# The compressed branch's softmax of a hybrid decoder layer: 32x32 block turns on VectorE in place of 128x128 transposes on TensorE

## The chip, the core and the metric

The kernel is one launch on one core of a Trainium2 chip. A core has five engines that run their own instruction streams: TensorE (PE, matrix products from SBUF into PSUM; its weight loads are listed as PEld), VectorE (DVE), ScalarE (ACT), GpSimd (POOL) and SyncE (SP), which here only issues transfers (DMAs). The streams are tied together by semaphores alone. The metric is the device time of the launch in microseconds (us), as a median over runs; less is better.

## What is computed

The layer takes `x` (512 tokens, 1024 channels), projects it once to 5912 columns, runs two token mixers on the result, gates and merges them, projects back and normalises. Mixer B is a gated linear recurrence (HGRN2) in chunks. Mixer A is a sparse attention of 8 heads in 2 groups, with three branches that share the queries: a compressed branch, a selected branch and a window branch. The change touches the compressed branch. There the keys and values of 32 tokens at a stride of 16 are squeezed by a small network into 31 compressed keys and values, and each query attends to those whose block has ended:

```python
def masked_softmax(s, mask):
    s = jnp.where(mask, s.astype(jnp.float32), -jnp.inf)
    m = jnp.max(s, axis=-1, keepdims=True)
    m = jnp.where(jnp.isfinite(m), m, 0.0)
    p = jnp.exp(s - m)
    d = jnp.sum(p, axis=-1, keepdims=True)
    return p / jnp.where(d > 0, d, 1.0)
...
        sc = jnp.einsum('bghqd,bgnd->bghqn', qn, kc) * scale
        pc = masked_softmax(sc, cmp_end[None, :] <= t[:, None])
        o_cmp = jnp.einsum('bghqn,bgnd->bghqd', pc.astype(vc.dtype), vc)
...
        return gt[..., 0:1] * o_cmp + gt[..., 1:2] * o_slc + gt[..., 2:3] * o_win
```

`gt` are the sigmoid gates per token, head and branch. With 512 tokens every block of the selected branch is taken, so both other branches are full causal attention over 512 keys here.

## The kernel before

**Products.** Each fp32 operand is split into a high part, rounded to the format `fp32r`, and the low rest, and a product is three matmuls: high by high, high by low, low by high. The high part is a cast on ACT, the low part a subtraction on DVE (`split2`, line 171; `split_steps`, line 176; the weights in `weights`, lines 249 to 255: the cast at line 251, the subtraction at line 254). A projection tile (`proj`, line 296) is 24 matmuls of 512 columns; its weights come by one DMA of 512 KB into one of two `wraw` buffers, asked for three tiles ahead (`load`), and split two tiles ahead.

**Order.** The order of the work is written out by hand with a counter. `_Weave` (line 75) holds a list of running chains, each a Python generator. Every projection calls `weave.tick()` four times, so that a tick stands for six matmuls, and each chain whose time has come emits its next piece and says by `yield n` in how many ticks it goes on. A piece that a chain emits stands ahead of the tick's six matmuls. The numbers `n` are the table `D` (line 70). `claim(ticks)` (line 97) keeps two PSUM-hungry pieces apart: a chain that claims holds the weave for so many ticks, and the next one that wants to claim polls until then. The instructions of TensorE and all the DMAs on SP keep this program order. Those of DVE and ACT, except a few, are ordered when the program is built.

**Tiles in order.** Ticks are counted here from the first `proj_i` (line 884): ticks 0 to 15 are the four value tiles of mixer B, 16 to 87 the tiles of `SEQ` (line 39; four ticks each, the `v` pair eight), 88 to 151 the sixteen merge gates, and 152 to 183 the eight branch tiles (`BRANCH`, line 47). Then come the output products without ticks.

**Full attention.** `attn_scores` (line 671) works in units `u`: query block i = 3, 2 with one branch each, then i = 1, 0 with both, in two halves of heads (`ms`). Each half claims `e0` ticks, issues its score matmuls, has the masking (line 702) done by DVE and starts `soften` (line 710): the exponentials on ACT (line 718), after `e1` ticks the division and the gates (lines 723 to 738), after `e3` and `t0` the 32x32 turns on DVE (line 746) into `big`. After the second half and `t3` ticks 16 DMAs (line 757) move the turned blocks across partitions into `turn`, and `t1` ticks later a chain `values` (line 764) starts for each block of 128 keys, `t4` ticks apart. It casts the high part on ACT into one of three `t4` buffers, subtracts on DVE (both by `split_steps`, lines 177 and 179, `y` ticks apart), and `t2` ticks later issues four matmuls into `pso`. One unit must be spent before the next unit's 16 DMAs are issued (line 750).

**Compressed branch.** `cmp_scores` (line 623) computes the scores with the 32 keys (31 and an empty one) on partitions, four heads below each other, and the 512 queries along the free dimension, for two groups `g`. Both results are copied to SBUF, by ACT (line 634) and by DVE (line 635). `cmp_probs` (line 640), once for each group, claims, turns the scores to queries on partitions by four 128x128 transposes on TensorE (`transpose4`, line 385), adds the mask (line 645), does the softmax along the 32 keys and multiplies by the gate over the sum, claims again, turns back by four more transposes and copies the result to SBUF (line 664). `attn_sum` (line 793) waits for both groups, claims, multiplies with the compressed values and adds the branches.

**Gates.** `gates` (line 579) turns the gate logits of tokens on partitions into `gat`, and multiplies the compressed branch's by `rvalid`, which is 0 for the first 31 queries, which see no compressed key.

**Turning for RoPE.** `rope` (line 591) moves each query or key tile by four DMAs of 64 KB, on SP.

Of the kernel before, what the change touches and what calls it, by code (L numbers as in the profile page):

```python
# [9 lines left out]
F32 = mybir.dt.float32  # L10
# [3 lines left out]
ALU = mybir.AluOpType  # L14
# [4 lines left out]
P = 128  # L19
KT = DM // P  # L20
NEG = -1.0e30
# [28 lines left out]
def _columns(name):  # L50

    c = np.arange(_COLS[name], _COLS[name] + 128)
    if name[0] == "q" and name[1] != "b" or name[:2] == "za":
# [9 lines left out]
O_END = O_PEV + 16  # L63


K_ID, K_TRI, K_CM, K_RV, K_SM, K_COS, K_SIN, K_MASK, K_END = (
    0, 128, 256, 384, 388, 900, 1412, 1924, 2436)


D = dict(h0=6, h2=5, h3=14, h4=0, h5=7, h6=8, n0=6, n1=3, n2=4, c0=1, c1=3, c2=4, c3=3, r0=5, p0=5, p1=6, p2=2, s0=5,  # L70
         s2=11, s3=2, v0=10, v1=11, v2=5, v3=9, e0=4, e1=2, t0=5, t1=5, t2=4, t3=2, t4=1, a5=1, y=2, w0=1, w1=3,
         x0=0, x1=1, e2=0, e3=2, o0=2, o1=6, o2=4)


class _Weave:
# [32 lines left out]
def layer_kernel(ctx: ExitStack, tc: tile.TileContext, xT, xn, w0, wi, wf, wv, small, brow, consts,  # L108
                 w1, w2, wbr, wout, lng, lnb, out):
    nc = tc.nc  # L110
    V, A, G = nc.vector, nc.scalar, nc.gpsimd
# [13 lines left out]
    cst = ctx.enter_context(tc.tile_pool(name="cst", bufs=1))  # L125
    strm = ctx.enter_context(tc.tile_pool(name="strm", bufs=3))
    come = ctx.enter_context(tc.tile_pool(name="come", bufs=2))
    t2 = ctx.enter_context(tc.tile_pool(name="t2", bufs=59))
    t4 = ctx.enter_context(tc.tile_pool(name="t4", bufs=3))
# [8 lines left out]
    def T2(n=512, dt=F32):  # L138
        return t2.tile([P, n], dt, name="t2", tag="t2")
# [10 lines left out]
    def SM(n, name):  # L150
        return sm.tile([P, n], F32, name="sm_" + name, tag="sm")
# [4 lines left out]
    def PS():  # L156
        return pss.tile([P, 512], F32, name="pss", tag="pss")

    def PT():
        return pst.tile([P, 512], F32, name="pst", tag="pst")  # L160
# [15 lines left out]
    def split_steps(src, dst_hi, dst_lo):  # L176
        A.copy(dst_hi, src)  # L177
        yield D["y"]
        V.tensor_tensor(dst_lo, src, dst_hi.bitcast(F32), ALU.subtract)  # L179
# [14 lines left out]
    con = cst.tile([P, K_SM], F32, name="con")  # L194
# [50 lines left out]
    def split_later(i):  # L245
        if i < len(order) and i not in parts:
            weave.start(weights(i), D["w0"])

    def weights(i):
        hi = strm.tile([P, 1024], F32R, name="whi", tag="whi")  # L250
        A.copy(hi, raws[i])  # L251
        yield D["w1"]
        lo = strm.tile([P, 1024], F32R, name="wlo", tag="wlo")
        V.tensor_tensor(lo, raws[i], hi.bitcast(F32), ALU.subtract)  # L254
        parts[i] = hi, lo
# [6 lines left out]
        dma(t, consts[:, K_SM + 512 * i:K_SM + 512 * i + 512])  # L262
    ident = con[:, K_ID:K_ID + 128]
    tri = con[:, K_TRI:K_TRI + 128].bitcast(I32)
    cmask = con[:, K_CM:K_CM + 128].rearrange("p (i n) -> p i n", n=32)
    rvalid = con[:, K_RV:K_RV + 4]

    def bias(m):
# [18 lines left out]
    for m in range(4):  # L287
        s = T2()
# [5 lines left out]
    weave = _Weave()  # L294

    def proj(name):
        i = M_INDEX[name]
        load(i + 3)
        split_later(i + 2)
        hi, lo = parts[i]  # L300
        ps = PA()
        for kt in range(KT):
            if kt % 2 == 0:
                weave.tick()
            c = slice(128 * kt, 128 * kt + 128)
            T.matmul(ps, hi[:, c], xh[kt], start=kt == 0, stop=False)
            T.matmul(ps, hi[:, c], xl[kt], start=False, stop=False)
            T.matmul(ps, lo[:, c], xh[kt], start=False, stop=kt == KT - 1)
        return ps, 4 + i
# [26 lines left out]
    def proj_v():  # L336
# [3 lines left out]
        for tt in range(4):  # L340
            c = slice(128 * tt, 128 * tt + 128)
            ps = PA()
            for kt in range(KT):
# [9 lines left out]
                T.matmul(ps[:, 0:NV], xl[kt][:, c], hi, start=False, stop=kt == KT - 1)  # L353
            weave.start(values_of(tt, ps), D["x0"])
            if tt == 1:
# [4 lines left out]
    def values_of(tt, ps):  # L360
        v = T2(NV)
        V.tensor_tensor(v, ps[:, 0:NV], brv, ALU.add)
        yield D["y"]
        vd = vv[:, tt].rearrange("p b (g c) -> p b g c", c=64)
        v4 = v[:, 0:256].rearrange("p (b g c) -> p b g c", b=2, c=64)
        G.tensor_copy(gat[:, tt], v[:, 256:NV])
        vts.append(vv[:, tt])
        yield from split_steps(v4, vd[:, :, 0:4:3], vd[:, :, 1:3])
# [13 lines left out]
    def chunks(ap):  # L382
        return ap.rearrange("p (t c s) -> p t c s", c=2, s=64)

    def transpose4(src, n=4):
        ps = PT()
        for j in range(n):
            T.transpose(ps[:, 128 * j:128 * j + 128], src[:, 128 * j:128 * j + 128], ident)
        return ps
# [22 lines left out]
    def hgrn(h):  # L412
# [11 lines left out]
        for w, e in ((1, e2), (0, e1)):  # L424
            V.tensor_tensor(chunks(e), cm[:, w].unsqueeze(3).to_broadcast([P, 4, 2, 64]), bc, ALU.subtract)
        yield D["h2"]
        qp = T2()
# [109 lines left out]
    mvs, ready = [None, None], set()  # L537
# [37 lines left out]

    gat = cst.tile([P, 4, 24], F32, name="gat")
    gv = gat.rearrange("p i (h b) -> p i h b", b=3)

    def gates():
        while len(vts) < 4:  # L580
            yield 1
        gflat = gat.rearrange("p i c -> p (i c)")
        A.activation(gflat, gflat, AF.Exp, scale=-1.0)
        yield 1
        V.tensor_scalar(gflat, gflat, 1.0, 2.0, ALU.add, ALU.mult)
        V.reciprocal(gflat, gflat)
        V.tensor_tensor(gv[:, :, :, 0], gv[:, :, :, 0], rvalid.unsqueeze(2).to_broadcast([P, 4, 8]), ALU.mult)
        ready.add("gates")


    def rope(raw):
# [29 lines left out]
    PTc = {}  # L621

    def cmp_scores():

        while "cmp" not in ready or len(qraw) < 4:
            yield 1
        yield from weave.claim(2)
        pg = PS(), PS()
        for m in range(4):
            for g in range(2):  # L630
                gs = slice(64 * g, 64 * g + 64)
                T.matmul(pg[g][32 * m:32 * m + 32], kcB[gs], qraw[m][gs], start=True, stop=True)
        sT = T2(), T2()
        A.copy(sT[0], pg[0])
        V.tensor_copy(sT[1], pg[1])
        yield D["p2"]
        for g in range(2):
            weave.start(cmp_probs(g, sT[g]), 2 * g)

    def cmp_probs(g, src):  # L640
        yield from weave.claim(2)
        ps = transpose4(src)
        s = T2()
        s3 = s.rearrange("p (x n) -> p x n", n=32)
        V.tensor_tensor(s.rearrange("p (i m n) -> p i m n", i=4, n=32),
                        ps.rearrange("p (i m n) -> p i m n", i=4, n=32),
                        cmask.unsqueeze(2).to_broadcast([P, 4, 4, 32]), ALU.add)
        mx = SM(16, "mx")
        V.tensor_reduce(mx, s3, AX.X, ALU.max)
        V.tensor_tensor(s3, s3, mx.unsqueeze(2).to_broadcast([P, 16, 32]), ALU.subtract)  # L650
        A.activation(s, s, AF.Exp, scale=0.125)
        yield D["p0"]
        while "gates" not in ready:
            yield 1
        V.tensor_reduce(mx, s3, AX.X, ALU.add)
        V.reciprocal(mx, mx)
        mxm = mx.rearrange("p (i m) -> p i m", i=4)
        V.tensor_tensor(mxm, mxm, gv[:, :, 4 * g:4 * g + 4, 0], ALU.mult)
        V.tensor_tensor(s3, s3, mx.unsqueeze(2).to_broadcast([P, 16, 32]), ALU.mult)
        yield D["p1"]  # L660
        yield from weave.claim(2)
        ps = transpose4(s)
        PTc[g] = T2()
        A.copy(PTc[g], ps)


    units = [(i, brs) for i in range(3, -1, -1) for brs in (((0,), (1,)) if i >= 2 else ((0, 1),))]
# [219 lines left out]
    for name, after in zip(SEQ, SEQ[1:] + [""]):  # L887
# [5 lines left out]
        ps, m = proj(name)  # L893
# [67 lines left out]
    for i in range(8):  # L961
        for c in "ab":
            name = "g%s%d" % (c, i)
# [4 lines left out]
    y, rb = {}, {}  # L968
# [13 lines left out]
    for n, (mix, m0) in enumerate(BRANCH):  # L982
        i = len(M_TILES) + n
# [7 lines left out]
        for m in (m0, m0 + 1):  # L991
            ps = (PA, PS)[m % 2]()
            for kt in range(4):
# [3 lines left out]
                c = slice(512 * (m - m0) + 128 * kt, 512 * (m - m0) + 128 * kt + 128)  # L997
# [6 lines left out]
    for hf in range(2):  # L1004
        n = slice(512 * hf, 512 * hf + 512)
# [56 lines left out]
    for u, (hf, a, b) in enumerate(((0, 0, 512), (1, 0, 256))):  # L1062
        ps = PS()[:, 0:b - a]
# [7 lines left out]
    ps = PT()[:, 0:256]  # L1071
# [16 lines left out]
def _constants():  # L1088
    c = np.zeros((128, K_END), np.float32)
    p = np.arange(128)  # L1090
    c[:, K_ID:K_ID + 128] = np.eye(128)
    c[:, K_TRI:K_TRI + 128] = p[:, None] <= p[None, :]
    n = np.arange(32)
    for i in range(4):
        t = 128 * i + p
        c[:, K_CM + 32 * i:K_CM + 32 * i + 32] = np.where(
            (16 * n[None, :] + 31 <= t[:, None]) & (n[None, :] < 31), 0.0, NEG)
        c[:, K_RV + i] = t >= 31
    c[:, K_SM:K_SM + 512] = np.arange(512) % 64 != 0
    inv = (np.float32(10000.0) ** (-np.arange(0, 64, 2, dtype=np.float32) / np.float32(64))).astype(np.float32)  # L1100
    ang = np.arange(512, dtype=np.float32)[None, :] * inv[p % 32][:, None]
    c[:, K_COS:K_COS + 512] = np.cos(ang)
    c[:, K_SIN:K_SIN + 512] = np.sin(ang) * np.where(p % 64 < 32, -1.0, 1.0)[:, None]
    c[:, K_MASK + 384:K_MASK + 512] = np.where(p[None, :] <= p[:, None], 0.0, NEG)
    return c
# [61 lines left out]
```

## Time and profile before

| quantity | value |
|---|---|
| time, median of 3 runs | 422.61 us (422.53 to 423.26) |
| time of the profiled execution | 421.37 us |
| its span in the profile | 419.6 us |
| TensorE busy | 408.2 us, 97% of the span |
| VectorE busy | 312.7 us, 75% |
| ScalarE busy | 239.1 us, 57% |
| GpSimd busy | 4.6 us, 1% |
| granted TensorE clock | 1.0 |

The span runs from the first to the last instruction that the profile shows; the time of the execution has 1.77 us more around it, and the median of the runs lies 1.24 us above the profiled execution. The profile gives, for every engine, each instruction with its start, its length, the tile that it writes and those that it reads (`out<-in`) and the source line. All matmuls have the helper's line 116 and all transposes line 120, so they are told apart by their tiles. Where an engine was idle before an instruction, the brackets behind the row give the idle time and what ended it. A row of windows gives the busy time of each engine in a stretch. Matmuls overlap: what one costs is read from start to start, not from its length.

### The profile page before, as it was taken

To read this page: it belongs to the slowest core of one execution; us is meant where nothing else is said; L and a number is where in the kernel's file an instruction comes from. 1 tells how busy PE (TensorE), PEld (TensorE's weight loads), DVE (VectorE), ACT (ScalarE), POOL (GpSimd) and SP (SyncE) were. 2 spreads that over 40 slices of the span, in tenths; PEclk is the share of its full clock that TensorE was granted. 3 is DMA by queue.
4 is the path that set the end of the run, shared out by engine and by line. 5 is a ranking of instruction groups with operands and counts; after the bars stand their busy time and mean duration, and the time that the engine had idled before them with its cause. 6 is when DMAs were issued, how large, how long until landed. Compare 5 with 4: busy or idle time off the path is not lost.

```text
span 419.6 us, 5940 instructions
## 1 busy us (share of the span) xinstructions
PE 408.2 (97%) x2063; PEld 333.9 (80%) x2063; DVE 312.7 (75%) x640; ACT 239.1 (57%) x469; POOL 4.6 (1%) x18
## 2 busy tenths in 40 slices
PE   9999999999999999999997999999999999899994
PEld 8888888898888777877785778788788778688884
DVE  5916498796777679799969669489682699992673
ACT  3445543724347575595578657666882787366301
POOL 2000000001000000000000000000000000000000
PEclk9999999999999999999999999999999999999999
DMA  7975902223342315931480641724854854035031
GB/s 260 372 231 201 309 3 66 89 76 100 91 135 77 94 59 175 206 122 50 124 227 15 190 149 63 184 104 123 230 164 129 275 199 137 1 104 199 15 137 51
DMA packets 25630, 58.05 MB, mean 138 GB/s; under 512 B 4480, under 2 KB 6400, under 8 KB 25600
## 3 DMA queue, kind: packets, MB, share of 16 engines
q1 hardware_dynamic: 25168, 57.28, 44.1%
q10 hardware_dynamic: 432, 0.39, 0.3%
q8 instruction: 16, 0.26, 0.3%
q14 instruction: 14, 0.11, 0.1%
HBM read 41.93 MB, written 2.10 MB: 105 GB/s over the span
## 4 chain that ended last, share of the span: by engine, by line
PE 84%; DVE 7%; SPq 3%; ACT 3%; DMA 2%; issue 1%; DVEq 0%; ACTq 0%
PE pa L116 55%; PE pso L116 12%; PE pss L116 12%; PE pst L116 5%; SPq L123 3%; ACT t L718 2%; DMA wraw<-in_wbr_dram 2%; DVE big L746 1%; DVE wlo L254 1%; DVE t L943 1%; PE pst L120 1%; DVE asum L788 1%; DVE t L787 1%; DVE t L179 1%; DVE asum L817 1%
## 5 line engine op out<-in xcount | busy, mean ns | idle before, releaser
L116 PE MATMUL pa<-t,whi 128*128 128x512 f32 x640 | 201.0, 395 | 1.9 <-DVE sm_nm L930 1.5
L116 PEld LDWEIGHTS pa<-t,whi 128*128 128x128 f32 x640 | 117.6, 188 | 32.8 <-issue 7.7
L116 PE MATMUL pa<-t,wlo 128*128 128x512 f32 x320 | 124.9, 390 | 0.0
L254 DVE TENSOR_TENSOR wlo<-wraw,whi 128x1024 fp32r<-128x1024 f32 x44 | 53.6, 1219 | 31.2 <-ACT whi L251 30.2
L116 PEld LDWEIGHTS pa<-t,wlo 128*128 128x128 f32 x320 | 60.1, 188 | 13.0
L251 ACT CAST whi<-wraw 128x1024 fp32r<-128x1024 f32 x44 | 46.1, 1047 | 29.2 <-PE pa L116 19.7
L718 ACT ACTIVATE t<-t,sm_mn 128x512 f32<-128x512 f32 (+3 forms) x64 | 35.1, 551 | 22.7 <-DVE sm_mn L702 22.7
L116 PE MATMUL pso<-t,t 128*128 128x512 f32 (+2 forms) x158 | 33.6, 349 | 0.0
L116 PE MATMUL pss<-t,t 128*128 128x512 f32 (+2 forms) x158 | 30.6, 324 | 0.0
L179 DVE TENSOR_TENSOR turn<-turn,t 128x1024 fp32r<-128x1024 f32 x20 | 23.6, 1218 | 8.8 <-DMA t<-in_wout_dram 6.5
L116 PEld LDWEIGHTS pso<-t,t 128*128 128x128 f32 x158 | 26.1, 197 | 3.9
L746 DVE STREAM_TRANSPOSE big<-t 128x512 f32<-128x512 f32 (+2 forms) x48 | 25.7, 591 | 2.8 <-PE pss L116 1.8
L116 PE MATMUL pa<-t,t 128*128 128x512 f32 (+1 forms) x104 | 27.2, 366 | 0.0
L116 PEld LDWEIGHTS pss<-t,t 128*128 128x128 f32 x158 | 23.9, 190 | 2.8
L177 ACT CAST t<-turn 128x1024 fp32r<-128x1024 f32 x20 | 20.1, 1046 | 6.9 <-DMA turn<-big 6.1
L116 PEld LDWEIGHTS pa<-t,t 128*128 128x128 f32 x104 | 18.3, 188 | 3.1
L702 DVE CUSTOM_DVE_ANT_0 t<-pss,t 128x512 f32<-128x512 f32 (+3 forms) x32 | 14.1, 487 | 8.5 <-PE pss L116 8.4
L116 PE MATMUL pa<-turn,t 128*128 128x512 f32 x64 | 19.9, 389 | 0.0
L116 PE MATMUL pss<-t,whi 128*128 128x512 f32 x64 | 19.7, 389 | 0.0
L734 ACT ACTIVATE t<-t,sm_dn 128x512 f32<-128x512 f32 (+3 forms) x32 | 15.8, 555 | 5.9 <-DVE sm_dn L726 5.9
L116 PE MATMUL pso<-turn,vv 128*128 128x512 f32 x40 | 16.0, 399 | 2.0 <-DVE turn L179 2.0
L177 ACT CAST t<-t 128x512 fp32r<-128x512 f32 x16 | 9.8, 615 | 13.4 <-DVE t L976 11.4
(202 smaller groups left out, 566.9 us busy)
## 6 DMA issues: line engine op xcount, KB each, us to landing
wraw<-in_wf_dram SPq DMA_DIRECT2D x38, 512.0 KB, 3.5
turn<-big SPq DMA_DIRECT2D x48, 128.0 KB, 2.4
wraw<-in_wbr_dram SPq DMA_DIRECT2D x8, 512.0 KB, 4.1
t<-in_wout_dram SPq DMA_DIRECT2D x16, 256.0 KB, 4.3
t<-t SPq DMA_DIRECT2D x48, 64.0 KB, 2.0
turn<-big SPq DMA_DIRECT2D x32, 96.0 KB, 2.2
t<-in_wi_dram SPq DMA_DIRECT2D x8, 256.0 KB, 5.6
big<-in_w_dram SPq DMA_DIRECT2D x8, 256.0 KB, 6.0
```

The lines of the kernel that those rows point to most:

```text
L116: return tc.keep_in_program_order(nc.tensor.matmul(*a, **k))
L120: return tc.keep_in_program_order(nc.tensor.transpose(*a, **k))
L123: tc.keep_in_program_order(nc.sync.dma_start(o, i))
L177: A.copy(dst_hi, src)
L179: V.tensor_tensor(dst_lo, src, dst_hi.bitcast(F32), ALU.subtract)
L251: A.copy(hi, raws[i])
L254: V.tensor_tensor(lo, raws[i], hi.bitcast(F32), ALU.subtract)
L702: V.tensor_tensor_reduce(out=p[:, c], in0=dsts[m, ab][:, c], in1=amask[:, 512 - n:512], op0=ALU.add, op1=ALU.min, scale=-0.125, scalar=3.0e38,
L718: A.activation(p[:, c], p[:, c], AF.Exp, bias=mn[:, h:h + 1], scale=-1.0, accum_out=den[:, h:h + 1])
L734: A.mul(ts[m, ab][:, c], ts[m, ab][:, c], den[:, h:h + 1])
L746: V.transpose(view[:, :, :, 4 * ab + m], ts[m, ab][:, 0:128 * nst].rearrange("p (c b s) -> p c b s", b=4, s=32))
L787: V.tensor_tensor(o[own], o[own], acc[ab][own], ALU.add)
```

## The change

Four things are changed; the rest of the kernel stays.

- The mask is stored with keys on partitions and queries along the free dimension (512 columns in place of 128). It isn't part of `con` any more: `cmp_scores` loads it by one DMA of 256 KB, and DVE adds it to the scores as it takes them from PSUM, in place of the two copies.
- `cmp_probs` turns the scores by `V.transpose`, which turns each 32x32 block of the tile in its place. The 32 keys of a head then lie along the free dimension, and the 32 queries of a block on partitions. Both `transpose4` and both claims go, and so does ACT's copy at the end: the turn back writes `PTc` straight.
- In this layout a row holds other tokens than before, so the gates are needed in another place: `gates` writes the compressed branch's gates to `gq` in the order of heads, and 16 DMAs of 32 partitions by 8 numbers move them to `gc`.
- Most delays of the table `D` are others.

```diff
-K_ID, K_TRI, K_CM, K_RV, K_SM, K_COS, K_SIN, K_MASK, K_END = (
-    0, 128, 256, 384, 388, 900, 1412, 1924, 2436)
+K_ID, K_TRI, K_RV, K_SM, K_COS, K_SIN, K_MASK, K_CM, K_END = (
+    0, 128, 256, 260, 772, 1284, 1796, 2308, 2820)
-D = dict(h0=6, h2=5, h3=14, h4=0, h5=7, h6=8, n0=6, n1=3, n2=4, c0=1, c1=3, c2=4, c3=3, r0=5, p0=5, p1=6, p2=2, s0=5,
-         s2=11, s3=2, v0=10, v1=11, v2=5, v3=9, e0=4, e1=2, t0=5, t1=5, t2=4, t3=2, t4=1, a5=1, y=2, w0=1, w1=3,
-         x0=0, x1=1, e2=0, e3=2, o0=2, o1=6, o2=4)
+D = dict(h0=6, h2=5, h3=14, h4=0, h5=7, h6=9, n0=5, n1=2, n2=2, c0=1, c1=3, c2=5, c3=4, r0=5, p0=0, p1=12, p2=0,
+         s0=3, s2=3, s3=3, v0=5, v1=11, v2=5, v3=9, e0=4, e1=2, t0=5, t1=4, t2=5, t3=3, t4=0, a5=4, y=2, w0=3, w1=1,
+         x0=0, x1=0, e2=0, e3=3, o0=1, o1=4, o2=0)
...
+    gq = cst.tile([P, 4, 8], F32, name="gq")
+    gc = cst.tile([P, 4, 8], F32, name="gc")
 
     def gates():
...
-        V.tensor_tensor(gv[:, :, :, 0], gv[:, :, :, 0], rvalid.unsqueeze(2).to_broadcast([P, 4, 8]), ALU.mult)
+        V.tensor_tensor(gq.rearrange("p m (g i) -> p m g i", g=2),
+                        gv[:, :, :, 0].rearrange("p i (g m) -> p m g i", g=2),
+                        rvalid.unsqueeze(1).unsqueeze(1).to_broadcast([P, 4, 2, 4]), ALU.mult)
         ready.add("gates")
+        for a in range(4):
+            for m in range(4):
+                dma(gc[32 * m:32 * m + 32, a], gq[32 * a:32 * a + 32, m])
+            yield 2
+        ready.add("cgates")
...
-        sT = T2(), T2()
-        A.copy(sT[0], pg[0])
-        V.tensor_copy(sT[1], pg[1])
+        sT, cmask = (T2(), T2()), T2()
+        dma(cmask, consts[:, K_CM:K_CM + 512])
         yield D["p2"]
         for g in range(2):
+            V.tensor_tensor(sT[g], pg[g], cmask, ALU.add)
             weave.start(cmp_probs(g, sT[g]), 2 * g)
 
     def cmp_probs(g, src):
-        yield from weave.claim(2)
-        ps = transpose4(src)
-        s = T2()
+        s, mx = T2(), SM(16, "mx")
         s3 = s.rearrange("p (x n) -> p x n", n=32)
-        V.tensor_tensor(s.rearrange("p (i m n) -> p i m n", i=4, n=32),
-                        ps.rearrange("p (i m n) -> p i m n", i=4, n=32),
-                        cmask.unsqueeze(2).to_broadcast([P, 4, 4, 32]), ALU.add)
-        mx = SM(16, "mx")
+        V.transpose(s, src)
         V.tensor_reduce(mx, s3, AX.X, ALU.max)
         V.tensor_tensor(s3, s3, mx.unsqueeze(2).to_broadcast([P, 16, 32]), ALU.subtract)
+        yield D["y"]
         A.activation(s, s, AF.Exp, scale=0.125)
         yield D["p0"]
-        while "gates" not in ready:
+        while "cgates" not in ready:
             yield 1
         V.tensor_reduce(mx, s3, AX.X, ALU.add)
         V.reciprocal(mx, mx)
-        mxm = mx.rearrange("p (i m) -> p i m", i=4)
-        V.tensor_tensor(mxm, mxm, gv[:, :, 4 * g:4 * g + 4, 0], ALU.mult)
+        mxi = mx.rearrange("p (i a) -> p a i", a=4)
+        V.tensor_tensor(mxi, mxi, gc[:, :, 4 * g:4 * g + 4], ALU.mult)
         V.tensor_tensor(s3, s3, mx.unsqueeze(2).to_broadcast([P, 16, 32]), ALU.mult)
         yield D["p1"]
-        yield from weave.claim(2)
-        ps = transpose4(s)
         PTc[g] = T2()
-        A.copy(PTc[g], ps)
+        V.transpose(PTc[g], s)
```

More of the change, by code (lines that the diff above doesn't have):

```diff
@@ L264, in layer_kernel @@
     tri = con[:, K_TRI:K_TRI + 128].bitcast(I32)
-    cmask = con[:, K_CM:K_CM + 128].rearrange("p (i n) -> p i n", n=32)
     rvalid = con[:, K_RV:K_RV + 4]
@@ L1092, in _constants @@
     c[:, K_TRI:K_TRI + 128] = p[:, None] <= p[None, :]
-    n = np.arange(32)
+    t, n = np.arange(512)[None, :], p[:, None] % 32
+    c[:, K_CM:K_CM + 512] = np.where((16 * n + 31 <= t) & (n < 31), 0.0, NEG)
     for i in range(4):
[L1095 to L1098, printed above, removed]
+        c[:, K_RV + i] = 128 * i + p >= 31
     c[:, K_SM:K_SM + 512] = np.arange(512) % 64 != 0
```

## The prediction

> **What bounds the kernel now.** I read the page's busy times and chain first, then the windows (stretch, length, busy time of PE, PEld, DVE, ACT, POOL, granted clock), then TensorE's own waits.
>
> ```profile
> span 419.6 us, 5940 instructions
> PE 408.2 (97%) x2063; PEld 333.9 (80%) x2063; DVE 312.7 (75%) x640; ACT 239.1 (57%) x469; POOL 4.6 (1%) x18
> PE 84%; DVE 7%; SPq 3%; ACT 3%; DMA 2%; issue 1%; DVEq 0%; ACTq 0%
> ```
> ```profile
> 180.00:200.00 20.00, 20.00 (x107) 15.20 (x106) 19.99 (x39) 15.64 (x29) 0.00 (x0) 1.00 0.23 82
> 200.00:215.00 15.00, 15.00 (x78) 12.09 (x77) 14.48 (x37) 10.76 (x24) 0.00 (x0) 1.00 0.62 155
> 221.00:228.00 7.00, 4.05 (x16) 2.57 (x15) 6.93 (x13) 6.50 (x9) 0.00 (x0) 1.00 0.00 0
> 318.00:330.00 12.00, 12.00 (x54) 9.70 (x53) 3.96 (x5) 3.83 (x8) 0.00 (x0) 1.00 0.69 198
> 345.00:372.00 27.00, 25.15 (x110) 20.22 (x109) 26.48 (x44) 15.97 (x31) 0.00 (x0) 1.00 0.21 70
> ```
> ```profile
> PE pso L116 <- DVE turn L179: 2.0, 1, 2.0
> PE pa L116 <- DVE sm_nm L930: 1.5, 1, 1.5
> PE pso L116 <- ACT t L177: 0.9, 1, 0.9
> PE pa L116 <- DVE t L972: 0.3, 1, 0.3
> ```
>
> TensorE is busy for 97% of the span and makes 84% of the chain. So the time falls only where TensorE gets less work or waits less. It is idle for 419.6 - 408.2 = 11.4 us, and two places in the middle hold 4.8 of these: 7.00 - 4.05 = 2.95 us at 221 to 228, where the products of turned blocks (`pso`) wait for ACT's cast and DVE's subtraction, and 27.00 - 25.15 = 1.85 us at 345 to 372, where branch products wait for DVE. VectorE counts only there, but it is full in the stretch of the change: 34.47 of the 35 us from 180 to 215.
>
> **Part 1: the sixteen transposes.**
>
> ```profile
> L120 PE MATMUL pst<-con,t x29: 270/272/273, 84.6 to 229.6; 128*128 128x128 f32 x29
> ...
> 203.49 0.60 PE L120 MATMUL pst<-con,t 128*128 128x128 f32 x4
> 203.84 0.71 PE L116 MATMUL pa<-t,whi 128*128 128x512 f32 x2
> 204.39 0.40 PE L116 MATMUL pa<-t,wlo 128*128 128x512 f32 x1
> 204.62 0.62 PE L116 MATMUL pa<-t,whi 128*128 128x512 f32 x2
> 205.08 0.39 PE L116 MATMUL pa<-t,wlo 128*128 128x512 f32 x1
> ```
>
> Of the 29 transposes 12 belong to the recurrence and one to the compression; 16 go, in four groups of four. From start to start a group holds TensorE for 203.84 - 203.49 = 0.35 us, and the next pair takes 204.39 - 203.84 = 0.55 in place of 205.08 - 204.62 = 0.46: 0.44 in all. Four groups: **-1.8 us**. This lies on the path wherever TensorE is full, so nothing hides it.
>
> The Trainium skill, "VectorE: DVE Perf Modes", section "The three transpose paths", puts a 128x128 transpose (in bf16) at 390 ns on TensorE against 311 ns on VectorE. By this, an estimate, 16 x 0.39 = 6.2 us would leave TensorE; the start-to-start row says 0.09 to 0.11 each, since transposes overlap, and I go by the row.
>
> **Part 2: VectorE and ScalarE.**
>
> ```profile
> L746 DVE STREAM_TRANSPOSE big<-t 128x512 f32<-128x512 f32 x24 | 15.2, 681 | 1.9 <-PE pss L116 1.8
> ```
> ```profile
> 187.58 0.66 DVE L635 COPY t<-pss 128x512 f32<-128x512 f32 x1
> ```
>
> VectorE gets four turns at 0.68 and loses one copy at 0.66; the mask's addition, the maxima, sums and products keep their sizes: +2.1 us in a stretch with 0.5 us free. ScalarE loses three copies. None of this is TensorE's, but all that DVE does behind it comes up to 2 us later. I take +0.5 for waits that this makes on TensorE (between 0, if slack covers it, and 2.1).
>
> **Part 3: the transfers.**
>
> ```profile
> L587 DVE TENSOR_TENSOR gat<-gat,con x1: 203/203/203, 101.5 to 101.5; 128x32 f32<-128x32 f32 x1
> ```
> ```profile
> 105.52 2.41 SPq L123 DMA_DIRECT2D t<-t  x4
> ...
> 112.92 2.79 SPq L123 DMA_DIRECT2D t<-t  x4
> ```
> ```profile
> 180.00 1.02 SPq L123 DMA_DIRECT2D wraw<-in_wf_dram  x2
> ...
> 192.68 0.33 SPq L123 DMA_DIRECT2D wraw<-in_wf_dram  x1
> ```
> ```profile
> t<-in_consts_dram SPq DMA_DIRECT2D x4, 256.0 KB, 7.6
> ```
>
> The sixteen gate transfers start when line 587 is through, at 101.7. Four issues take SP 2.4 us, as for the 64 KB ones; that 1 KB issues like 64 KB is an estimate. In program order come four gates, the RoPE turns of q0 (105.52 before), eight gates, those of q1 (112.92), four gates. From 101.7: 104.1; q0's at their old time to 107.9; eight gates to 112.7; a weight load of 0.5; q1's at 113.3 for 112.92. So +0.4 us on q1's turned copy, which VectorE may absorb: 0. If the issues took twice as long, q1 and the first scores would be some 5 us late; that is the upper end. The gates have 80 us until they are used.
>
> The mask's transfer is emitted at the tick of the compressed scores, behind a weight load that went at 180 to 181 and ahead of the one that waited until 192.68. Landing takes up to 7.6 us (the slowest of this size): 189 at the latest, against the copy at 187.58 that the addition replaces. VectorE loses 0 to 1.5 us; in Part 2's term.
>
> **Part 4: the delays.** A tick is six matmuls of 0.23 us (204.62 - 204.39), 1.37 us. Counting ticks from the first `proj_i`: the second half of u = 0 is scored at 56, u = 1 at 65 and 74, the compressed scores come at 78 and u = 2 at 83, before and after. Then the transposes' claims are gone: the scores that stood at 89, 95, 101, 108 and 119 stand at 88, 93, 100, 105 and 116, with `attn_sum` at 97 for 105. For u = 1, 74 + 1 + e1 + e3 + t0 + t3 gives the 16 DMAs at 86 before and 88 after, and the products at 98 and 100: each block has 12 ticks from DMAs to products in both. What decides is SP.
>
> ```profile
> 203.06 0.33 SPq L123 DMA_DIRECT2D wraw<-in_wf_dram  x1
> 203.49 11.79 SPq L123 DMA_DIRECT2D turn<-big  x16
> ```
> ```profile
> turn<-big SPq DMA_DIRECT2D x48, 128.0 KB, 2.4
> ```
> ```profile
> 206.88 1.22 DVE L254 TENSOR_TENSOR wlo<-wraw,whi 128x1024 fp32r<-128x1024 f32 x1
> ```
> ```profile
> 222.36 2.92 ACT L177 CAST t<-turn 128x1024 fp32r<-128x1024 f32 x3
> ...
> 226.73 1.05 ACT L177 CAST t<-turn 128x1024 fp32r<-128x1024 f32 x1 [0.50 <-PE pso L116]
> ```
> ```profile
> 224.73 3.45 DVE L179 TENSOR_TENSOR turn<-turn,t 128x1024 fp32r<-128x1024 f32 x3
> ```
> ```profile
> 223.44 0.50 PE L116 MATMUL pso<-t,vv 128*128 128x512 f32 x1 [0.92 <-ACT t L177]
> ...
> 225.97 0.50 PE L116 MATMUL pso<-turn,vv 128*128 128x512 f32 x1 [2.03 <-DVE turn L179]
> ```
>
> Before, the last of u = 1's DMAs landed at 215.28 + 2.4 = 217.7, but the cast began at 222.36, behind the exponentials of the scores at 95, and TensorE, at tick 98, waited 2.95 us. After, those scores stand at 93, so their exponentials are out of the way. But the DMAs at tick 88 come behind the weight load of the tile that starts there, whose buffer is free when the subtraction at 206.88 is done: 208.1 + 11.8 + 2.4 = 222.3, and 222.3 + 1.05 + 1.15 = 224.5 for the first block. TensorE reaches tick 100 at 222.4 (tick 98 without its wait) + 2.7 - 1.3 (three groups of transposes) + 2.5 (`attn_sum` and a half of scores, now ahead) = 226.3. The slack is 1.8 us. I keep 0.75 of the 2.95 as a remainder: **-2.2 us** (from -2.95 to +2).
>
> With t4 = 0 all four blocks of a unit are multiplied in one tick, but there are three `t4` buffers: the fourth cast waits for the first block's four products, as at 226.73. It then needs 1.05 + 1.15 = 2.2 us while TensorE has eight products, 1.9 us, to do: 0.3, with semaphores 0.5, for each of three units with four blocks (u = 0, 1, 4): **+1.0**, counting u = 1 half since its remainder stands above (0 to 3).
>
> ```profile
> L943 DVE SCALAR_TENSOR_TENSOR t<-t,sm_nm,t 128x512 fp32r<-128x512 f32 x16 | 11.3, 749 | 0.0
> ```
>
> At 345 to 372 VectorE is full (26.48 of 27), with these 11.3 us of output weights in the way, while it was idle for 8.0 of the 12 us at 318 to 330. The waits of o0, o1, o2 fall from 12 to 5 ticks and x1 to 0, and the last unit's DMAs come 3 ticks earlier (143 for 146), so this work moves forward into that hole: **-1.3** of the 1.85 (0 to -1.85). The final waits behind tick 183 stay.
>
> **Sum.** -1.8 + 0.5 - 2.2 + 1.0 - 1.3 = -3.8 us against the profiled 421.37: 417.6. The median of the runs lies 422.61 - 421.37 = 1.24 above it, so I predict **418.8**, 0.9% less.
>
> **Rivals.** (a) Only the transposes count: the stalls at 221 and 345 come back at other ticks, with the same 4.8 us; 422.61 - 1.8 = 420.8. For it: 25 new delays only shift work about where engines are full. Against: both stalls have a cause that the new order removes. Chance 0.2.
>
> (b) The gain is cancelled: the transposes' 1.8 us are eaten by the fourth block's waits (+1.5) and VectorE's extra work (+0.5); 422.6. Chance 0.09.
>
> (c) Slower: the turned blocks come later than their products. Place: SP's queue, where u = 1's DMAs stand behind the weight load that needs the subtraction at 206.88. VectorE is full there and gets 2.1 us more. With a lateness L over 1.8 us TensorE waits L - 1.8, at all four blocks at once; u = 4 has the same twelve ticks and the same order on SP. With both late, the waits at the end kept and u = 0 in time as before, the sum is -1.8 + 0.5 + 1.0 - 2.95 + 2 x (L - 1.8), which turns slower at L = 3.4; at 4.5 it is +2.2, 424.8. For it: the full windows. Against: u = 0 and 4 showed no wait before. Chance 0.13.
>
> The Trainium skill, "TensorE: Matmul & The Clock Gate", section "HAM oscillation — how this bites in real kernels", holds that an idle gap over some 3.4 us halves TensorE's clock; a stall of (c) would then cost up to another 2 us, an estimate. The trace shows 1.00 through the 2.95, which came in two pieces.
>
> **How the numbers follow.** Forecast 0.58 (its own terms: 417.0 to 420.4), (a) 0.2, (b) 0.09, (c) 0.13. A measurement tells 0.2%, 0.85 us, from no change. Faster: the forecast and (a), less a little of (a) that ends near the edge: 0.76; same 0.1; slower 0.14. The range runs from 416.6, where both stalls go and no wait is added (-1.8 - 2.95 - 1.3), to 422.9, where (b) ends; it leaves out (c) and a better case.
>
> **What would show it.** TensorE with 2047 matmuls and 13 transposes, and some 1.8 us less busy. No `pso` wait over 1 us near tick 100; a cast of u = 1's blocks within a microsecond of landing. A fourth block's `pso` waiting a few tenths. VectorE some 2 us busier in all, with line 943 ahead of 345. The prediction is wrong if TensorE waits for line 179 or 177 for over 3 us in sum, for `gc`, or at the first scores.

## The result, and the profile after

| quantity | before | after |
|---|---|---|
| median of the runs compared | 422.57 us (4 runs) | 416.61 us (4 runs, 416.12 to 416.96) |
| ratio, 95% interval | | 0.9858, 0.9839 to 0.9878 |
| profiled execution | 421.37 us | 416.12 us |
| its span | 419.6 us | 414.3 us |

The change made the kernel faster by 6.0 us, to 416.61 us; 418.8 us was forecast. The direction was right, and the forecast gain was too small. One execution of the first experiment's kernel took 467.16 us at a granted clock of 0.84, where its others took 429.9 to 432.7, and is left out there. From the page after (span, busy times, shares of the chain of waits):

```profile
span 414.3 us, 5920 instructions
PE 405.7 (98%) x2047; PEld 331.7 (80%) x2047; DVE 314.4 (76%) x641; ACT 237.5 (57%) x466; POOL 4.6 (1%) x18
PE 84%; DVE 8%; ACT 3%; DMA 2%; SPq 1%; issue 1%; DVEq 0%; ACTq 0%
```

TensorE has the 2047 matmuls that were forecast and is 2.5 us less busy; its idle time fell from 11.4 to 414.3 - 405.7 = 8.6 us. TensorE's own waits after (releaser, sum, times, longest), and the transposes that are left:

```profile
PE pso L116 <- DVE t L189: 1.0, 1, 1.0
PE pso L116 <- DVE turn L179: 0.8, 2, 0.4
PE pa L116 <- ACT t L962: 0.7, 1, 0.7
```
```profile
L120 PE MATMUL pst<-con,t 128*128 128x128 f32 x13 | 2.2, 272 | 0.0
```

The wait of 1.0 is that of the very first matmul, the same before. The waits for L177, L930 and L972 are gone; new is one for a gate tile on ScalarE (L962). Windows of after (stretch, length, busy times of PE, PEld, DVE, ACT and POOL, granted clock, DMA share, GB/s), at the places that answer to 221 to 228, 318 to 330 and 345 to 372 of before:

```profile
224.00:235.00 11.00, 10.60 (x50) 7.43 (x49) 10.50 (x16) 7.53 (x9) 0.00 (x0) 1.00 0.22 81
318.00:330.00 12.00, 12.00 (x55) 9.86 (x54) 5.73 (x7) 8.21 (x17) 0.00 (x0) 1.00 0.81 259
339.00:366.00 27.00, 27.00 (x120) 22.27 (x120) 26.97 (x45) 17.81 (x36) 0.00 (x0) 1.00 0.27 84
```

TensorE is idle for 0.40 us instead of 2.95 around u = 1's products, and never in the last stretch, though VectorE is as full there as before. The balance was taken on TensorE: for every matmul the time from its start to the next one's start, less the median of that for its shape; what is over is a gap, put down to its place.

| place on TensorE | before | after | difference |
|---|---|---|---|
| sixteen transposes, with the change of shape behind each four | 1.8 | 0 | -1.8 |
| u = 1's first block (1.08 and 2.30 before) | 3.4 | 0.2 | -3.2 |
| branch products (0.50 and 1.66) | 2.2 | 0 | -2.2 |
| fourth blocks of u = 0, 1, 4 (0.24, 0.57, 0.58 after) | 0 | 1.4 | +1.4 |
| gate tile on ScalarE, L962, at 291 | 0.2 | 0.9 | +0.7 |
| sum | | | -5.1 |

The profiled executions differ by 5.25 us. The medians differ by 5.96, because the median of the four runs lies 1.20 us above the profiled execution before and 0.49 us above it after.

### The profile page after: what moved, and what is told of

It is laid out like the page before. It is cut to its first block, busy times and chain, and to the rows that moved or that the text cites. A ratio compares the mean times of both kernels' runs of the same rounds, so it can differ in the third digit from the quotient of the medians.

```text
span 414.3 us, 5920 instructions
## 1 busy us (share of the span) xinstructions
PE 405.7 (98%) x2047; PEld 331.7 (80%) x2047; DVE 314.4 (76%) x641; ACT 237.5 (57%) x466; POOL 4.6 (1%) x18
## 4 chain that ended last, share of the span: by engine, by line
PE 84%; DVE 8%; ACT 3%; DMA 2%; SPq 1%; issue 1%; DVEq 0%; ACTq 0%
PE pa L116 55%; PE pss L116 15%; PE pso L116 9%; PE pst L116 5%; DVE turn L179 4%; DVE big L750 2%; DMA wraw<-in_wf_dram 2%; ACT t L722 2%; SPq L123 1%; DVE wlo L254 1%; ACT t L177 1%; DMA turn<-big 1%; PE pst L120 0%; DVE asum L792 0%; DVE t L791 0%
## 5 line engine op out<-in xcount | busy, mean ns | idle before, releaser
L179 DVE TENSOR_TENSOR turn<-turn,t 128x1024 fp32r<-128x1024 f32 x20 | 23.4, 1215 | 8.0 <-DMA t<-in_wout_dram 5.0
L177 ACT CAST t<-turn 128x1024 fp32r<-128x1024 f32 x20 | 19.9, 1047 | 6.9 <-DMA turn<-big 6.0
L962 ACT ACTIVATE t<-pa,hbias 128x512 f32<-128x512 f32 x16 | 10.9, 679 | 10.7 <-PE pa L116 10.7
```

The lines of the kernel that those rows point to most:

```text
L962: A.activation(gm[name], ps, AF.Tanh, bias=hbias[:, m:m + 1], scale=0.5)
```

## Experiments

Each of the sixteen kernels was timed in five rounds beside the kernel before, and the ratios are to that. The kernel before had medians of 421.71 to 422.38 us there, so differences under 1 us between two experiments are not read. The delays are written as they stand in the table `D`.

**Half of the change alone.** First the new code with all old delays, then the old code with all new delays.

```diff
-D = dict(... all delays of after ...)
+D = dict(... all delays of before ...)
```

> The changed code with every delay of the table D as it was before: the softmax on VectorE and the gate transfers alone. Theory A (the freed claims do it): without the transposes' claims the scores of u = 3 move ahead, their exponentials no longer stand before u = 1's casts, so the 3.4 us wait at the products of u = 1 goes along with the 1.9 us of transposes, while the waits in the branch products (2.2 us) stay: about 417.5. Rival B (the new delays do it): only the transposes count, the wait of 3 to 3.4 us at u = 1 stays: about 420.7.

Measured: 431.89 us, ratio 1.0211 (1.018 to 1.0242), over 10 us above both expectations. TensorE's own waits in this run:

```profile
PE pso L116 <- DVE turn L179: 6.5, 5, 2.6
PE pso L116 <- ACT t L177: 2.9, 4, 1.5
PE pa L116 <- ACT t L962: 1.4, 1, 1.4
PE pso L116 <- DVE t L189: 1.1, 1, 1.1
```

> The kernel before with the new table D alone, the transposes and their claims kept. Theory A: the claims still push the scores, the wait at u = 1 stays (2 us or more), the waits in the branch products go (-2.2), the fourth block's waits come (+1.6): about 422. Rival B: both waits go, the fourth block's come: -3.4 - 2.2 + 1.6 + 0.7, about 419.3.

Measured: 440.94 us, ratio 1.0439 (1.041 to 1.0468), again far above both expectations. Either half alone is slower than the 422.28 us of the kernel before in these rounds, by 9.6 and 18.7 us, and together they gain 6. So the change isn't a sum of parts, as the prediction had it. In the first, u = 1's blocks still come late (gaps of 0.89 and 2.82 us at 221 to 225) and u = 3's as well (1.7 and 2.3 us at 282); in the second, u = 0's blocks are late by 3.2 and 4.3 us at 191, and a branch product waits for 5.1 us at 361 (for L179, not for the lines L930 and L972 of before).

**The tail's delays.**

```diff
-x1=0, o0=1, o1=4, o2=0
+x1=1, o0=2, o1=6, o2=4
```

> The changed kernel with o0, o1, o2 and x1 as before (2, 6, 4, 1). If the earlier splitting of the output weights is what took the waits out of the branch products, they come back: +2.2, about 418.8. Rival: the last unit's earlier end did it, and nothing comes back: 416.6.

Measured: 417.03 us, ratio 0.9871 (0.9847 to 0.9895), and no wait of branch products. The output weights' subtractions run at 343 to 353 again, as before, and nothing waits. These four delays don't explain the 2.2 us that went.

**A fourth buffer for the blocks' high parts.**

```diff
-    t4 = ctx.enter_context(tc.tile_pool(name="t4", bufs=3))
+    t4 = ctx.enter_context(tc.tile_pool(name="t4", bufs=4))
```

(with two buffers fewer in `t2`, for the space)

> The changed kernel with four t4 buffers in place of three (and 57 t2 buffers in place of 59, to make room). If the waits of 0.24, 0.57 and 0.58 us before the fourth block's low product come from the missing buffer, they go: -1.4, about 415.2. Rival: the fourth block is late because ACT and DVE take the four one after the other, and a buffer changes little: 416.4.

Measured: 419.5 us, ratio 0.9937 (0.9912 to 0.9961), above both expectations. The fourth blocks' waits went, which confirms their cause, but there are gaps of 1.4, 1.9 (for 0.9) and 1.7 us at 86, 292 and 345. Whether these come from the fourth buffer or from the two that `t2` lost was not separated.

**The turned blocks' delays**, first new among old ones, then old among new ones, in the new code.

```diff
-e3=2, t1=5, t2=4, t3=2, t4=1
+e3=3, t1=4, t2=5, t3=3, t4=0
```

> The changed code with the old table D but for the five delays between the scores of a unit and its products (e3, t1, t2, t3, t4), which are new. Theory C: with the softmax on VectorE the old five put the products of a unit before its turned blocks are cast, and the loss of the softmax alone (432.1) is theirs: with the new five most of the 15.4 us between 432.1 and 416.6 comes back, 417 to 420. Rival D: the split of the weights (w0, w1) or another delay is what the softmax needs: 428 to 432.

Measured: 426.09 us, ratio 1.0075 (1.0046 to 1.0103). That is between the two expectations. The waits at u = 1 and u = 3 of the run with all delays old are gone; what is left is mainly waits for the gate tile L962, 3.6 us at 286 and 2.5 at 324, and one of 1.1 us for u = 4's fourth block.

> The changed kernel with only these five delays as before. Theory C: the waits of 3 to 6 us at the products of u = 1 and of i = 2 come back, with the halved clock behind them: 424 to 432. Rival D: little changes, 416 to 418.

Measured: 430.47 us, ratio 1.0187 (1.0161 to 1.0212). u = 1's blocks are late again (0.7 and 3.0 us), u = 3's too (3.3 and 2.0). So the new softmax needs this group. Without it blocks come later than their products, as in rival (c) of the prediction, but not from its place, SyncE's queue: the last of u = 1's transfers had landed at 220.0, and ScalarE's cast began only at 222.96, behind other work in its list.

**The weights' splits.**

```diff
-w0=3, w1=1
+w0=1, w1=3
```

> The changed kernel with w0 = 1 and w1 = 3, as before: the cast of the weights' high part two ticks earlier in ACT's order, the subtraction at the same tick. Theory C: 416 to 418. Rival D: the casts stand ahead of the turned blocks' casts on ACT and the waits at the products come back, 422 to 430.

Measured: 416.16 us, ratio 0.9853 (0.9829 to 0.9877): no effect.

**Transposes back on TensorE,** first of the data that VectorE turns, then of the identity matrix, ready from the start. VectorE's turns stay, and what TensorE makes is not read.

```diff
         V.transpose(s, src)
+        transpose4(src)
...
         V.transpose(PTc[g], s)
+        transpose4(s)
```

> The changed kernel with four transposes on TensorE put back behind each of the four turns on VectorE; nobody reads what they write. If a group costs TensorE 0.44 us and all else keeps its place, +1.8 us: 418.4. If they cost more by holding PSUM banks that the scores need, over 419; if the figure of 0.39 us for each holds, +6.2, 422.8.

Measured: 424.94 us, ratio 1.0062 (1.0038 to 1.0087), 8.3 us over the changed kernel: over the 419 of the second expectation, but not for its reason, PSUM banks. TensorE in that run waits for VectorE, and the window behind the wait shows a clock of 0.50:

```profile
PE pst L120 <- DVE t L645: 3.5, 1, 3.5
```
```profile
189.45 0.39 PE L116 MATMUL pa<-t,wlo 128*128 128x512 f32 x1
193.29 0.85 PE L120 MATMUL pst<-con,t 128*128 128x128 f32 x4 [3.45 <-DVE t L645]
```
```profile
194.20:196.50 2.30, 2.30 (x6) 1.73 (x6) 2.30 (x4) 0.00 (x0) 0.00 (x0) 0.50 0.21 34
```

```diff
-        transpose4(src)
+        transpose4(con, step=0)
```

(four times the first 128 columns of `con`, and the same behind the second turn)

> The changed kernel with sixteen further transposes on TensorE, four behind each turn on VectorE as in the run with unread transposes, but of the identity matrix, which is ready from the start; their result is not read. Theory (the transposes' own price is small, their due time is dear): the kernel before shows 0.11 us each, so the profile shows 0.35 to 0.45 us per group, no new wait at 189 and 1.8 us in all: 418.4, ratio 0.990. Rival (the price was in TensorE's order of work itself, a weight load or a PSUM buffer at that place): a wait of some us at the same places, 422 or more. Second rival (a transpose of ready data is hidden beside the neighbours' weight loads): 416.6, nothing.

Measured: 419.03 us, ratio 0.9936 (0.9903 to 0.997), 2.4 us over the changed kernel; the span is 416.4, 2.1 us over its 414.3, and from start to start each group again takes 0.35 us with 0.1 behind it. That is the price of sixteen transposes in TensorE's time. The other 5.9 us of the run before were no price of transposes in themselves: TensorE takes its instructions in order, and in the new schedule VectorE adds the mask 8 us after the scores. With the softmax on VectorE nothing on TensorE has to wait for it until `attn_sum`.

**More groups of delays,** each back to its old values in the changed kernel.

```diff
-a5=4
+a5=1
```

> The changed kernel with the attention's wait ahead of the branch products (a5) back from 4 to 1. Theory (the waits of branch products at 345 to 357 went because TensorE's earlier waits are gone and the turned blocks of the last unit come in time, not by this wait): no wait over 0.5 us behind 340, time within 1 us of 416.6, ratio 0.984 to 0.988. Rival (a5 keeps the four products of attention and gate from VectorE's queue while it needs L930 and L943, so it is what removed the two waits of 2.2 us): a wait of 0.5 to 2 us for VectorE comes back between 340 and 360, 418 to 419, ratio 0.990.

Measured: 417.73 us, ratio 0.9903 (0.9879 to 0.9928); 1.1 us over the changed kernel, with two gaps of 0.2 and 0.3 us at 343 and 346. It isn't what removed the 2.2 us either.

```diff
-c2=5, c3=4, p0=0, p1=12, p2=0, s0=3, s2=3, s3=3, v0=5
+c2=4, c3=3, p0=5, p1=6, p2=2, s0=5, s2=11, s3=2, v0=10
```

> The changed kernel with the delays of the compressed branch and of the scores' starts back (c2, c3, p0, p1, p2, s0, s2, s3, v0), those of the turned blocks, of the weights and of the tail kept new. Theory (the remaining 9.5 us of the run with only the turned blocks' delays new sit here: scores start later, so the last exponentials come later and the first gate tile behind them): TensorE waits for ScalarE's L962 some 3.5 us at 286 and 2.4 us at 324, each with a slow stretch behind it, about 425, ratio 1.005. Rival (those waits come from the first stages' delays h6, n0, n1, n2, or from a5): no wait for L962 over 1 us, 416 to 418, ratio 0.985 to 0.990.

Measured: 426.36 us, ratio 1.0109 (1.0082 to 1.0137). The waits came where they were expected, but not for the reason given. ScalarE around the last unit's exponentials, in the changed kernel and then in this one:

```profile
281.61 0.69 ACT L962 ACTIVATE t<-pa,hbias 128x512 f32<-128x512 f32 x1
285.56 0.40 ACT L722 ACTIVATE t<-t,sm_mn 128x128 f32<-128x128 f32 x1 [3.27 <-DVE sm_mn L706]
...
291.75 0.66 ACT L962 ACTIVATE t<-pa,hbias 128x512 f32<-128x512 f32 x1
```
```profile
283.36 0.40 ACT L722 ACTIVATE t<-t,sm_mn 128x128 f32<-128x128 f32 x1 [1.11 <-DVE sm_mn L706]
...
289.55 1.24 ACT L962 ACTIVATE t<-pa,hbias 128x512 f32<-128x512 f32 x2
```
```profile
286.45 0.39 PE L116 MATMUL pa<-t,wlo 128*128 128x512 f32 x1
290.26 0.73 PE L116 MATMUL pa<-t,whi 128*128 128x512 f32 x2 [3.43 <-ACT t L962]
```

The exponentials come 2.2 us earlier here, not later. But ScalarE's instructions stand in a fixed order that was made when the program was built: in the changed kernel one gate tile stands ahead of the sixteen exponentials and one behind; here both stand behind. The first one's PSUM bank comes free only after the sixteen (16 x 0.39 = 6.2 us), and TensorE, which needs that bank, waits for 3.4 us.

```diff
-t4=0
+t4=1
```

> The changed kernel with the wait between the products of one unit's blocks (t4) back from 0 to 1, so that a block's four products stand one tick apart. Theory (the fourth block's waits of 0.24, 0.57 and 0.58 us are the price of t4 = 0 with three buffers): all three are under 0.1 us, u = 1 shows no wait, 415.2 to 416.2, ratio 0.982 to 0.985. Rival (the blocks' products, three ticks later for the fourth, delay what stands behind them as the fourth buffer did, where new waits of 1.4 to 1.9 us came in other places): 417 to 420 with a new wait of over 1 us for ScalarE.

Measured: 444.13 us, ratio 1.0525 (1.0496 to 1.0555), a miss on both sides. ScalarE in this run:

```profile
224.88 0.69 ACT L962 ACTIVATE t<-pa,hbias 128x512 f32<-128x512 f32 x1 [1.82 <-PE pa L116]
227.55 0.61 ACT L722 ACTIVATE t<-t,sm_mn 128x384 f32<-128x384 f32 x1 [1.99 <-DVE sm_mn L706]
...
231.58 2.92 ACT L177 CAST t<-turn 128x1024 fp32r<-128x1024 f32 x3
```

In the changed kernel the cast of u = 1's blocks follows the gate tile L962 at once, at 225.82. Here ScalarE is idle for 2 us between them and then does a later unit's exponentials, which stand ahead of the cast: it comes 5.8 us later. Again the order, not the data, is late: the last transfer had landed at 223.8. TensorE waits for casts at three units.

**Is it the order?** The middle group's old delays, as above, with the last unit's exponentials emitted two ticks later, so that nine stand ahead of the gate tile; and the same, by four ticks, in the changed kernel.

```diff
     def soften(u, ms, ts, mn, den):
...
+        if u == 5:
+            yield 2
         for z, m in enumerate(ms):
...
-        yield D["t0"]
+        yield D["t0"] - (2 if u == 5 else 0)
```

> The changed kernel with the middle group's delays old, as in the run before last (426.4 us), and besides the exponentials of the last unit emitted two ticks later (their later wait two ticks shorter), so that ScalarE's list has the gate tile behind nine of the sixteen exponentials and not behind all. Theory (ScalarE's fixed order is the cause: the gate tile that TensorE needs for its free bank stands behind 16 exponentials of 0.39 us): nine end at about 286.9, the gate tile at 287.5, so the excess at 286 falls from 3.6 to 1.0 to 1.5 us, the slow stretch of 1.4 us behind it is gone, 422 to 423, ratio 0.999 to 1.003. Rival (TensorE waits there for something else that comes late with these delays): the gap stays over 3 us, 425 to 427.

Measured: 423.26 us, ratio 1.0019 (1.0001 to 1.0037). TensorE's gap at 286 is 0.9 us for 3.6:

```profile
287.59 0.73 PE L116 MATMUL pa<-t,whi 128*128 128x512 f32 x2 [0.73 <-ACT t L964]
```

Only the exponentials' place in the order was moved; the gap at 286 lost 2.7 us and the slow stretch behind it went, and the median fell by 3.1. The spans of the two profiled executions are nearer, 422.4 and 421.8 us: the first was the fastest of its seven runs, and in the second u = 4's first block waits for 1.5 us at 302, where there was no gap, and the gap at 324 (1.8) is 2.1 us at 322.

> The changed kernel with the exponentials of the last unit emitted four ticks later (their later wait four ticks shorter), so that ScalarE's list has the second gate tile behind nine of the sixteen exponentials. Theory (same cause): the wait of 0.9 us at 291 goes, 415.5 to 416.2, ratio 0.981 to 0.985. Rival (the exponentials' end moves back by one gate tile, 0.6 us, and the last unit's turns and transfers with it, so a wait of the same size comes at its products): 416.4 to 417.5.

Measured: 416.11 us, ratio 0.9859 (0.9832 to 0.9887). The wait at 291 is gone, but the fourth block of u = 4 waits 1.2 us for 0.6: the rival's mechanism; the time is the same.

```diff
-c2=5, c3=4
+c2=4, c3=3
```

> The changed kernel with only two delays old: the steps of the compression ahead of its second claim (c2 4, c3 3, for 5 and 4). They move the second scores of u = 1 and all that comes behind by one tick of 1.4 us, and in ScalarE's list the tenth gate tile falls behind the sixteen exponentials of the last unit. Theory (this order alone makes most of the 9.8 us of the middle group): a gap of 3 to 4 us at 286 with a slow stretch behind it, 421 to 426, ratio 0.997 to 1.010. Rival (one tick is absorbed, the scores' starts or the softmax's p delays make the 9.8 us): 416 to 418.

Measured: 426.59 us, ratio 1.01 (1.0072 to 1.0127), with the 3.6 us at 288. These two delays alone cost as much as the whole middle group. They stand ahead of the softmax, in the compression; they shift what follows by one tick of 1.4 us, and the gate tile falls behind the exponentials.

**Part 3 doubled.**

```diff
                 dma(gc[32 * m:32 * m + 32, a], gq[32 * a:32 * a + 32, m])
+                dma(gd[32 * m:32 * m + 32, a], gq[32 * a:32 * a + 32, m])
```

> The changed kernel with each of the sixteen gate transfers made twice, the second time into a tile that nobody reads. Theory (as in the prediction's Part 3: 0.6 us of SyncE's queue each, in a stretch where nothing on TensorE waits for SyncE): no new wait of TensorE, 416.2 to 417.0, ratio 0.983 to 0.988; the turned copies of the RoPE come about 5 us later on SyncE and are absorbed. Rival (the RoPE turns of q1 and with them the first scores of the next unit come late): a wait of 1 to 5 us between 112 and 145, 418 to 421.

Measured: 424.61 us, ratio 1.0054 (1.0034 to 1.0075): the rival. SyncE in the changed kernel, then SyncE and TensorE in this one:

```profile
101.48 2.41 SPq L123 DMA_DIRECT2D gc<-gq  x4
...
105.23 2.43 SPq L123 DMA_DIRECT2D t<-t  x4
107.70 5.02 SPq L123 DMA_DIRECT2D gc<-gq  x8
112.82 0.53 SPq L123 DMA_DIRECT2D wraw<-in_wf_dram  x1
113.44 2.41 SPq L123 DMA_DIRECT2D t<-t  x4
```
```profile
121.91 2.41 SPq L123 DMA_DIRECT2D t<-t  x4
```
```profile
125.69 0.49 PE L116 MATMUL pss<-kh,t 64*128 64x512 f32 x1
130.60 0.79 PE L116 MATMUL pss<-kh,t 64*128 64x512 f32 x1 [4.42 <-DVE t L469]
```

Twelve of the sixteen added issues, 0.6 us each, stand ahead of the turns of q1 and put them 8.5 us later, and the first scores wait 4.4 us. So the sixteen transfers of the change are free only because some 4 us (8.5 - 4.4) of slack lie behind them.

No run is measurably faster than the change itself: the intervals of 416.11, 416.16 and 416.61 lie over each other.

## Why the forecast was right in direction and wrong in size

The steps that failed are two terms of Part 4, u = 1's blocks and the tail, and the median's distance. The first had the wrong wait ("What decides is SP", where ScalarE's list decided) and came to -3.2 us for -2.2; the second had a reason that the runs refute and came to -2.2 for -1.3.

**Part 1, -1.8: right.** The balance gives -1.8, and the run with ready transposes +2.1 in the span. What the prediction didn't see is the other side of a transpose on TensorE: it binds TensorE's order to the softmax, and in the new schedule that would cost another 5.9 us.

**Part 2, +0.5: about right.** VectorE is 1.7 us busier, 2.1 were forecast. The one wait that may be due to it is that for the gate tile at 291, +0.7, behind exponentials that waited for VectorE. That VectorE's extra work is its cause was not shown.

**Part 3, 0: right, and its bound near.** The order on SyncE is the one written out, and q1's turns start at 113.44, forecast 113.3. The upper end, "if the issues took twice as long, q1 and the first scores would be some 5 us late", was near for the scores, though twelve issues of 0.6 us stand ahead of q1, which makes 7 us: with the transfers doubled q1's turns were 8.5 us late and TensorE stood still in the first scores for 4.4, and the slow stretch behind raised the price (below).

**Part 4, u = 1: the wait went, but not by the working.** "I keep 0.75 of the 2.95 as a remainder"; the balance has 0.2 left of 3.4, -3.2 in place of -2.2. SyncE, the landing of the last two transfers, ScalarE and TensorE in the changed kernel, with u = 1's transfers, casts and products:

```profile
211.57 10.28 SPq L123 DMA_DIRECT2D turn<-big  x16
```
```profile
DMA to landing us min/median/max: 2.6/2.6/2.7
```
```profile
225.23 0.69 ACT L962 ACTIVATE t<-pa,hbias 128x512 f32<-128x512 f32 x1 [1.82 <-PE pa L116]
225.82 2.93 ACT L177 CAST t<-turn 128x1024 fp32r<-128x1024 f32 x3
```
```profile
227.74 0.49 PE L116 MATMUL pso<-t,vv 128*128 128x512 f32 x1
228.17 0.50 PE L116 MATMUL pso<-turn,vv 128*128 128x512 f32 x1
...
232.03 0.50 PE L116 MATMUL pso<-turn,vv 128*128 128x512 f32 x1 [0.40 <-DVE turn L179]
```

The transfers stand behind the weight load, as forecast, though 3 us later; the last was issued at 221.27 and landed 2.7 us later, at 223.9, forecast 222.3. (A landing counts from the start of an issue; the prediction added it to the end.) The cast came 1.9 us after that, where "within a microsecond" was expected: it stands in ScalarE's list behind a gate tile, and ScalarE sat idle until TensorE had made that tile. So ScalarE's list decided, not SP, and the transfers had 1.9 us to spare. The first block was ready at 225.82 + 1.05 + 1.15 = 228.0, forecast 224.5. TensorE came later too, 227.7 for 226.3, in part since the count missed that the second scores of u = 1 move from tick 74 to 75, held by the compression's claim one tick later (c2, c3). The slack of 1.8 us that the text worked out was in fact none: the first block's low part came 0.2 us late. That so little was lost was luck: the runs with the old delays of this group show what lateness costs.

**Part 4, fourth blocks: right mechanism, +1.4 for +1.0.** The gaps are 0.24 for u = 0, 0.57 for u = 1, 0.58 for u = 4. The run with a fourth buffer (and two `t2` buffers fewer) had none of them and lost more elsewhere.

**Part 4, the tail: the gain came, the reason fell.** "So this work moves forward into that hole: -1.3"; measured -2.2. The work did move (its first subtractions at 334 for 348), but with o0, o1, o2 and x1 old it runs at 343 to 353 and nothing waits. Nor do a5, the middle group or the weights' splits bring the waits back. With the turned blocks' delays old there is a wait of 2.2 us at 353, but for another line (L179). Setting all delays back doesn't either: the new code with the old table has no gap over 0.1 us behind 325 and none of these waits in its list above. The old code with all new delays has none for these lines, though its branch products wait 5.1 us for L179. Both of these runs had lost time before that place, which may let VectorE get ahead, so they don't tell which half of the change removed the waits; that stays open.

**The median's distance: failed.** "The median of the runs lies 1.24 above it" was carried over from before; after it is 0.49. Of the miss of 2.2 us (418.8 - 416.6) this is 0.75. The terms make the rest, to within 0.2 us: u = 1 gave 1.0 more and the tail 0.9 more than forecast, the fourth blocks took 0.4 more and Part 2's wait 0.2 more.

**The rivals.** (a) and (b) fell: both stalls went, and what was added eats 2.1 of 7.2 us. (c) did not decide in the changed kernel. Its mechanism, blocks later than their products, is what the runs with half of the change and the one with this group old show, at 430 to 441 us where 424.8 was forecast for it. There the lateness arose on ScalarE's list and not on SyncE's queue (with all delays old the last of u = 1's transfers landed at 218.1 and the cast began at 221.4), and a slow stretch followed a wait.

## What to carry to other kernels

Where engines' orders are fixed when the program is built, a delay table isn't a list of independent costs: look for the one instruction that stands behind a burst (here a gate tile behind sixteen exponentials) and ask which side of the burst a shift of one tick puts it on. Price an operation on a full, in-order engine twice: by its time (0.11 us for a transpose here) and by what it makes the engine wait for (3.5 us here). When two parts of a change are each slower alone, only runs with one group of settings put back tell which of them carry the gain.

## What the runs showed of the hardware

After a wait, TensorE often ran at half speed for a while. Windows of the run with doubled gate transfers, and of that with the split exponentials on the middle group:

```profile
125.00:130.00 5.00, 1.18 (x5) 0.46 (x3) 3.50 (x6) 3.14 (x6) 0.00 (x0) 0.96 0.09 16
130.00:136.50 6.50, 5.90 (x18) 4.25 (x19) 4.71 (x13) 3.28 (x9) 0.00 (x0) 0.51 0.65 202
```
```profile
322.00:325.00 3.00, 1.03 (x5) 0.57 (x4) 2.36 (x2) 3.00 (x7) 0.00 (x0) 1.00 0.90 277
325.00:329.00 4.00, 4.00 (x13) 3.10 (x12) 1.65 (x3) 2.56 (x8) 0.00 (x0) 0.58 0.97 371
```

In the first, TensorE is busy for 5.9 us at a granted clock of 0.51 behind an idle gap of 4.4 us; by an estimate that loses 5.9 x 0.49 = 2.9 us, so the wait of 4.4 costs some 7. In the second a gap of 1.97 us was enough, and the clock fell 1.4 us after work had begun again. The Trainium skill, "TensorE: Matmul & The Clock Gate", section "HAM oscillation — how this bites in real kernels", puts the limit at some 3.4 us of idleness; the gaps of 3.4 us (the run with the middle group old) and 4.4 us here agree with it, that of 1.97 does not, and the kernel before kept 1.00 through gaps of 0.92 and 2.03 us close together, as the run with the middle group old did behind one of 1.7 us at 325. So in these runs the length of a gap alone doesn't tell whether the clock falls.
